# RWKV layer: the reversed copy of the values in DRAM made in two halves of eight column blocks, and the transposes of the key norms placed between two low-rank products

## The chip, the cores and the metric

The kernel runs on one core of one Trainium2 chip. The metric is the device time of one execution in microseconds (us). Three runs of the kernel before gave 2610.16, 2610.86 and 2616.23 us; the median is 2610.86 us.

## What is computed

One inference step of a four-layer backbone (retention, RWKV-7 time mixing, differential attention, neighbourhood attention) for 128 context tokens and 512 latent tokens, 640 in all, with 1024 channels in float32. Only the RWKV layer is touched. Cut to what matters, it is:

```python
r, k, v, g = einsum('nbld,dne->nble', stack([x_r, x_k, x_v, x_g]), w_in)   # x_* = h + (shift(h) - h) * mu[n]
kk = k * k_k
kk = kk * rsqrt(max(sum(kk * kk, -1), 1e-12))            # one root per token and head
for dr in range(2):                                      # forward and backward in time
    wlog = -softplus(-(w0[dr] + tanh(x_w @ wA[dr]) @ wB[dr])) - 0.5   # low-rank product
    a = sigmoid(a0[dr] + (x_a @ aA[dr]) @ aB[dr])                     # low-rank product
    kd = k * (1 + (a - 1) * k_a)
    seq = (r, exp(-exp(wlog)), kd, v, kk, a)
    if dr == 1:
        seq = tuple(flip(t, axis=time) for t in seq)     # the values are needed in reversed time too
    y_d, s_d = rwkv7_scan(*seq, s0[:, dr])
```

The values are needed twice: in the order of time for the forward scan, and reversed for the backward scan, apart for the 128 context tokens and the 512 latent tokens.

## The kernel before, in words

The RWKV layer has two stages. The first (`rwkv_project`, about 700 to 1180 us of the profile) makes the projections k, r, v and g in this order and stores them in DRAM; between k and r it makes the two low-rank products (`low_rank(1)` of tanh, `low_rank(4)`). The second (`rwkv_mix`) reads them back by pairs of heads and runs the scans in chunks of 64 tokens.

A projection goes through four column groups (`c2`, 256 columns each). Each group loads its weights in two DMAs of 512 KB (L160), which ScalarE (ACT) and VectorE (DVE) split into two parts each, and TensorE (PE) makes three products for each block of 128 inputs (L88 to L90). For the values, a group has five blocks of 128 tokens (`tt`); each result is copied by ACT from PSUM to one of two buffers `wvs` (L1149) and stored to the DRAM tensor `wd_v` (L1150). When the four groups of the values are done, two DMAs copy `wd_v` to `wd_vr` with reversed time, the 128 context tokens and the 512 latent ones apart (L1179). Both sides of the copy are seen as two column blocks of 512 columns (2 KB), the block first: 2 x 128 x 512 and 2 x 512 x 512. `wd_vr` is read by the second stage alone (L1477 to L1479).

The sums of squares of the keys land in a PSUM tile `wn` (L1173); DVE makes the roots (a tile of 128 x 80: 16 heads for each of five token blocks) in eleven small instructions (`rsqrt`, L124 to L129), PE turns them by five transposes (L1189), ACT copies them (L1190), and a DMA stores them to `wd_n` (L1191), from where each head pair reads its row into `wkk` (L1226) for the product in L1235.

While r, v and g are projected, a generator (`rwkv_prepare`, 8 steps, one per head pair) is fed into the same engines by priorities: it loads `wBr` (L1230), splits it into `wB` on ACT and DVE (L1232, L93), makes the decays, and stores `wd_bk`, `wd_q`, `wd_lt`, `wd_lb`; `rwkv_inverse` makes triangular inverses on DVE (L1310, L1312).

All engines run their instructions in a fixed order, which a scheduler works out from priorities and a simulated timeline; `high_priority()` moves what is inside it ahead. All DMAs are issued by SyncE (SP) in one order. A DMA's instruction waits in that order for its source and its target to be ready.

Of the kernel before, what the change touches and what calls it, by code (L numbers as in the profile page):

```python
# [7 lines left out]
F32 = mybir.dt.float32  # L8
# [10 lines left out]
NP = 128  # L19
# [1053 lines left out]
class Rwkv:  # L1073
    def rwkv_project(s, hT, dr):

        nc, I = s.nc, s.I
        v, act, pe, gp = nc.vector, nc.scalar, nc.tensor, nc.gpsimd
        s.pj_bufs, s.wz_bufs = 3, 2
        with s.pool(name='w1', bufs=1) as w1, s.pool(name='w1p', bufs=1, space=PSUM) as pp:
            s.pp = pp  # L1080
            T = lambda shape, name, bufs=1, dt=F32: w1.tile(shape, dt, name=name, tag=name, bufs=bufs)
            xx = T([128, 8, NT], 'wxx')

            for k, shape in (('wN', [80, 32, 32]), ('wX', [80, 32, 32]), ('wBK', [128, NCH, 128]), ('wQ', [128, 2, NCH, 64]),
                             ('wLT', [128, NCH, 64]), ('wt1', [128, NT]), ('wt2', [128, NT]), ('wt4', [128, NT])):
                T(shape, k, s.pbufs.get(k, 1))
            for a, b in PARTS:
                for g in range(0, 8, s.xx_g):
                    e = gp if s.xx_p[g // s.xx_g] == 'p' else v
                    lo, hi = max(a - 1, 1), b - 1  # L1090
                    G = slice(g, g + s.xx_g)
                    edge = lambda t, src: e.tensor_copy(xx[:, G, t:t + 1], hT[:, G, src:src + 1])
                    e.tensor_tensor(out=xx[:, G, lo:hi], in0=hT[:, G, lo - 1:hi - 1], in1=hT[:, G, lo + 1:hi + 1], op=ALU.add)
                    if a == 0:
                        edge(0, 1)
                        edge(NP - 1, NP - 2)
                        edge(NP, NP + 1)
                    else:
                        edge(NT - 1, NT - 2)
                    lo, hi = (0, hi) if a == 0 else (lo, NT)  # L1100
                    v.scalar_tensor_tensor(out=xx[:, G, lo:hi], in0=xx[:, G, lo:hi], scalar=0.5, in1=hT[:, G, lo:hi], op0=ALU.mult, op1=ALU.subtract)

            def mix(n, cuts=(0, NT)):
                parts = [(T([128, NT], 'wxh', s.x_bufs, F32R), T([128, NT], 'wxl', s.x_bufs, F32R)) for _ in range(8)]
                for a, b in zip(cuts, cuts[1:]):
                    for kc in range(8):
                        m = T([128, NT], 'wm', 2)[:, :b - a]
                        v.scalar_tensor_tensor(out=m, in0=xx[:, kc, a:b], scalar=s.vc('rwkv_mu', 8 * n + kc), in1=hT[:, kc, a:b],
                                               op0=ALU.mult, op1=ALU.add)
                        s.split(*(p[:, a:b] for p in parts[kc]), m, v)  # L1110
                return lambda kc, sl: (parts[kc][0][:, sl], parts[kc][1][:, sl])

            def low_rank(n, W, parts_, fn):
                x_ = mix(n)
                w = s.weights_list([W[0], W[1]])
                for hf in range(2):
                    ps = s.proj_T(w, 0, hf, x_)
                    t = T([128, HV], 'wlr')
                    act.activation(out=t, in_=ps, func=fn)
                    s.split(parts_[0][:, hf * HV:hf * HV + HV], parts_[1][:, hf * HV:hf * HV + HV], t)  # L1120

            W = I['rwkv_w_in'][0]
            nrm = pp.tile([128, 2, 512], F32, name='wn', tag='wn')

            for k, n in (('pj', s.pj_bufs), ('pm', 1), ('wz', s.wz_bufs)):
                for _ in range(n):
                    pp.tile([128, 512], F32, name=k, tag=k, bufs=n)
            prep = None

            def step(kind, c2):  # L1130
                for _ in range(s.preps.get(kind, (0, 0, 0, 0))[c2]):
                    with s.tc.high_priority(s.hp[4]):
                        next(prep)

            for n, base, kind in ((2, 1024, 'k'), (0, 0, 'r'), (3, 2048, 'v'), (5, 3072, 'g')):
                if kind == 'g' and s.rate:
                    s.fill_rest()
                x_ = mix(n, (0, HV, NT) if kind == 'k' else (0, NT))
                if prep is None:
                    s.tw = [T([128, NT], f'wtw{j}', 1, F32R) for j in range(2)]  # L1140
                    s.ta = [T([128, NT], f'wta{j}', 1, F32R) for j in range(2)]
                    prep = s.rwkv_prepare(w1, pp, dr)
                    next(prep)
                for c2 in range(4):
                    w = s.weights(W[:, base + c2 * 256:base + c2 * 256 + 256])
                    if kind == 'v':
                        for tt in range(5):
                            st = T([128, 256], 'wvs', 2)
                            act.copy(st, s.proj_N(w, tt, 256, x_))  # L1149
                            nc.sync.dma_start(out=dr['v'][tt * 128:tt * 128 + 128, c2 * 256:c2 * 256 + 256], in_=st)  # L1150
                        step('v', c2)
                        continue
                    sts = [T([128, NT], 'wst', 2) for _ in range(2)]
                    if kind == 'k':
                        sqs = [T([128, NT], k) for k in ('wt1', 'wt2')]
                    for hf in range(2):
                        for cc in range(2):
                            c, st = c2 * 2 + cc, sts[cc]
                            ps = s.proj_T(w, cc, hf, x_)
                            sl = slice(hf * HV, hf * HV + HV)  # L1160
                            if kind == 'g':
                                th = T([128, HV], 'wth')
                                act.activation(out=th, in_=ps, func=AF.Tanh, scale=0.5)
                                v.scalar_tensor_tensor(out=st[:, sl], in0=th, scalar=1.0, in1=ps, op0=ALU.add, op1=ALU.mult)  # L1164
                            else:
                                act.copy(st[:, sl], ps)
                                if kind == 'k':
                                    act.activation(out=sqs[cc][:, sl], in_=ps, func=AF.Square, scale=s.vc('rwkv_kk', c))
                    for cc in range(2):
                        if kind == 'k':  # L1170
                            c = c2 * 2 + cc
                            for tt in range(5):
                                pe.matmul(nrm[:, 0, tt * 16:tt * 16 + 16], sqs[cc][:, tt * 128:tt * 128 + 128], s.ind[:, c, :], start=c + tt == 0, stop=c + tt == 11)  # L1173
                        nc.sync.dma_start(out=dr[kind][c2 * 2 + cc], in_=sts[cc])
                    if kind in 'rg':
                        step(kind, c2)
                if kind == 'v':
                    for a, b in ((0, NP), (NP, NT)):
                        nc.sync.dma_start(out=dr['vr'][a:b].rearrange("t (a w) -> a t w", a=2),  # L1179
                                          in_=dr['v'][a:b].rearrange("t (a w) -> a t w", a=2)[:, ::-1])  # L1180
                if kind == 'k':
                    n2, y_, t_ = (T([128, 80], k) for k in ('wn2', 'wny', 'wnt'))
                    v.tensor_scalar(out=n2, in0=nrm[:, 0, :80], scalar1=1e-12, scalar2=None, op0=ALU.max)
                    rn = s.rsqrt(w1, n2, None, None, y_, t_)
                    rt = T([128, NT], 'wst', 2)[:16]
                    for a, b in ((0, 4), (4, 5)):
                        ps = pp.tile([128, 512], F32, name='pj', tag='pj', bufs=s.pj_bufs)
                        for tt in range(a, b):
                            pe.transpose(ps[:16, (tt - a) * 128:(tt - a) * 128 + 128], rn[:, tt * 16:tt * 16 + 16], s.ident)  # L1189
                        act.copy(rt[:, a * 128:b * 128], ps[:16, :(b - a) * 128])  # L1190
                    nc.sync.dma_start(out=dr['n'], in_=rt)  # L1191
                    with s.tc.high_priority():
                        low_rank(1, I['rwkv_wA'][0], s.tw, AF.Tanh)
                        low_rank(4, I['rwkv_aA'][0], s.ta, AF.Copy)

    def rwkv_prepare(s, pool, pp, dr):
# [649 lines left out]
```

## Time and profile before

| | us |
|---|---|
| median of three runs | 2610.86 |
| profiled execution | 2608.0 |
| its span | 2606.2 |
| PE busy / DVE busy / ACT busy | 2308.8 / 1500.5 / 1067.3 |
| mean granted clock of PE | 0.925 of full speed |

The page cuts the span into 40 slices of 65 us and gives each a digit of busy tenths. From slice 13 to slice 24 (782 to 1564 us) PE stands at 8 or 9 tenths, but for two: slice 17 (1042 to 1108 us) with 2 tenths of PE, 3 of DVE, 1 of ACT and a granted clock of 6 tenths, and slice 19 (1173 to 1238 us), where the second stage begins, with 4 tenths of PE and of DVE.

### The profile page before, as it was taken

The page shows a single profiled execution, that of the slowest core. Times are in us where ns is not written, and L with a number is a line of the kernel's source. Part 1 is how long each engine was busy: PE and PEld are TensorE (multiplying, and loading weights), DVE is VectorE, ACT ScalarE, POOL GpSimd, SP SyncE. Part 2 cuts the span into 40 slices and gives each one's busy share as a digit, 9 for nine tenths or more (in the row PEclk, how much of TensorE's full clock was granted, in tenths as well). Part 3 has the DMA queues.
Part 4 walks back from the last instruction along what each step waited for, and adds up shares of the span by engine and source line. Part 5 has one row for each costly group of instructions (what it writes and reads, how often), then busy time and mean ns, then how long its engine had stood idle before and what let it go on. Part 6 is the DMA issues. An engine that isn't in the chain of part 4 may idle for free.

```text
span 2606.2 us, 48698 instructions
## 1 busy us (share of the span) xinstructions
PE 2308.8 (89%) x18951; PEld 2086.3 (80%) x18951; DVE 1500.5 (58%) x3511; ACT 1067.3 (41%) x2405; POOL 675.5 (26%) x576
## 2 busy tenths in 40 slices
PE   7999999997988999294888997889889888999998
PEld 5888888987958889194777877688888887898888
DVE  7534343443173898394888554657776665645554
ACT  5323233332153655152333342245554433645551
POOL 3323232303210000001243433233222323332321
PEclk9999999998988889695888888899999998999999
DMA  8433333225272566367365645511111122223321
GB/s 294 131 101 102 118 101 110 90 85 188 83 262 69 166 191 216 107 193 182 102 148 136 160 126 177 175 56 48 45 55 39 51 68 56 67 76 78 77 71 57
DMA packets 344586, 303.54 MB, mean 116 GB/s; under 512 B 140220, under 2 KB 281044, under 8 KB 344356
## 3 DMA queue, kind: packets, MB, share of 16 engines
q1 hardware_dynamic: 344356, 300.44, 38.8%
q8 instruction: 149, 2.44, 0.4%
q14 instruction: 81, 0.66, 0.1%
HBM read 231.37 MB, written 64.79 MB: 114 GB/s over the span
## 4 chain that ended last, share of the span: by engine, by line
PE 34%; DVE 14%; DMA 4%; issue 3%; ACT 3%; SPq 3%; POOL 1%; ACTq 0%; DVEq 0%; POOLq 0%
PE pj L88 5%; PE pj L89 5%; PE pj L90 5%; PE oa L88 2%; PE oa L89 2%; PE oa L90 2%; DVE wtmp L1310 2%; DVE wX L1312 1%; PE nO L1024 1%; PE wsc L1439 1%; PE dtp L839 1%; PE wch L1507 1%; PE npt L1007 1%; PE wy L1541 1%; SPq L160 1%
## 5 line engine op out<-in xcount | busy, mean ns | idle before, releaser
L93 POOL TENSOR_TENSOR wl<-wr,wh 128x1024 fp32r<-128x1024 f32 (+1 forms) x168 | 371.2, 2222 | 628.5 <-ACT wh L170 490.4
L88 PE MATMUL pj<-hH,wh 128*128 128x320 f32 x1280 | 408.2, 321 | 10.5 <-ACT hH L96 7.1
L89 PE MATMUL pj<-hL,wh 128*128 128x320 f32 x1280 | 406.7, 318 | 3.0 <-POOL hL L93 2.4
L90 PE MATMUL pj<-hH,wl 128*128 128x320 f32 x1280 | 404.1, 316 | 0.1
L88 PEld LDWEIGHTS pj<-hH,wh 128*128 128x128 f32 x1280 | 246.4, 193 | 24.3 <-ACT hH L96 10.4
L89 PEld LDWEIGHTS pj<-hL,wh 128*128 128x128 f32 x1280 | 247.1, 193 | 10.6 <-POOL hL L93 3.8
L90 PEld LDWEIGHTS pj<-hH,wl 128*128 128x128 f32 x1280 | 246.5, 193 | 2.4 <-issue 1.0
L170 ACT CAST wh<-wr 128x1024 fp32r<-128x1024 f32 x168 | 175.5, 1047 | 133.7 <-PE pj L89 48.6
L88 PE MATMUL oa<-oh,wh 128*128 128x384 f32 (+1 forms) x640 | 201.6, 316 | 20.6 <-ACT wh L170 14.4
L89 PE MATMUL oa<-ol,wh 128*128 128x256 f32 (+1 forms) x640 | 199.3, 313 | 0.1
L88 PE MATMUL pj<-wh,hH 128*128 128x256 f32 x640 | 188.4, 294 | 12.2 <-DVE dr L756 7.4
L90 PE MATMUL oa<-oh,wl 128*128 128x256 f32 (+1 forms) x640 | 199.1, 312 | 0.0
L89 PE MATMUL pj<-wl,hH 128*128 128x256 f32 x640 | 186.0, 291 | 0.0
L90 PE MATMUL pj<-wh,hL 128*128 128x256 f32 x640 | 185.4, 290 | 0.0
L88 PE MATMUL pj<-wxh,wh 128*128 128x320 f32 x416 | 132.8, 327 | 53.2 <-DVE wst L1164 44.8
L88 PEld LDWEIGHTS pj<-wh,hH 128*128 128x128 f32 x640 | 127.5, 199 | 20.3 <-DVE dr L756 8.3
L88 PEld LDWEIGHTS oa<-oh,wh 128*128 128x128 f32 x640 | 122.8, 192 | 23.7 <-ACT wh L170 16.3
L89 PE MATMUL pj<-wxl,wh 128*128 128x320 f32 x416 | 134.5, 325 | 2.2 <-DVE wxl L93 2.2
L90 PE MATMUL pj<-wxh,wl 128*128 128x320 f32 x416 | 133.8, 323 | 1.9 <-DVE wl L93 1.9
L88 PEld LDWEIGHTS pj<-wxh,wh 128*128 128x128 f32 x416 | 82.1, 199 | 58.1 <-DVE wst L1164 45.1
L89 PEld LDWEIGHTS pj<-wl,hH 128*128 128x128 f32 x640 | 127.7, 200 | 0.0
L90 PEld LDWEIGHTS pj<-wh,hL 128*128 128x128 f32 x640 | 127.5, 199 | 0.0
(479 smaller groups left out, 5601.0 us busy)
## 6 DMA issues: line engine op xcount, KB each, us to landing
wr<-in_ret_w_in SPq DMA_DIRECT2D x48, 512.0 KB
wm<-in_w_mod SPq DMA_DIRECT2D x40, 512.0 KB
wr<-in_w_mod SPq DMA_DIRECT2D x32, 512.0 KB
wr<-in_rwkv_w_in SPq DMA_DIRECT2D x32, 512.0 KB
wl<-in_w_mod SPq DMA_DIRECT2D x24, 512.0 KB
wr<-in_diff_w_in SPq DMA_DIRECT2D x48, 256.0 KB
wr<-in_na_w_in SPq DMA_DIRECT2D x48, 256.0 KB
wd_bk<-wBK SPq DMA_DIRECT2D x16, 640.0 KB
```

The costliest lines, as they stand in the source:

```text
L88: mm(out, l[0], r[0], start=start, stop=False)
L89: mm(out, l[0], r[1], start=False, stop=False)
L90: mm(out, l[1], r[0], start=False, stop=stop)
L93: eng.tensor_tensor(out=lo, in0=src, in1=hi.bitcast(F32), op=ALU.subtract)
L160: nc.sync.dma_start(out=raw[:, :, c:c + x.shape[1]], in_=x[j * 128:(j + 4) * 128].rearrange("(k p) c -> p k c", p=128))
L170: nc.scalar.copy(hi[:, :, :n], raw[:, :, :n])
L839: pe.matmul(po, at[:, j * 128:j * 128 + 128], v_[:, vt, cc * 128:cc * 128 + 128], start=j == 0, stop=j == nt - 1)
L1007: pe.transpose(pt[:, j * 128:j * 128 + 128], P[:, j * 128:j * 128 + 128], s.ident)
L1024: pe.matmul(ot_ps[i * 64:i * 64 + 64, oc:oc + 128], vt[j][:, hc:hc + 64], pts[i][:, j * 128:j * 128 + 128], start=j == 0, stop=j == len(vt ...
L1310: v.tensor_tensor(out=t, in0=X_[:, 0:j + 1, j:j + 1].to_broadcast([80, j + 1, n]), in1=N_[:, j:j + 1, j + 1:].to_broadcast([80, j + 1, n]) ...
L1312: v.tensor_tensor(out=X_[:, 0:j + 1, j + 1:], in0=X_[:, 0:j + 1, j + 1:], in1=t, op=ALU.subtract)
L1439: pe.matmul(ps[:, u - u0, :], QT[:, u, :], TT[:, u, :], start=True, stop=True)
```

## The change

The copy to `wd_vr` is made in two halves of 512 columns: the first when the groups 0 and 1 of the values are done, the second when the groups 2 and 3 are done. Each half is seen as eight column blocks of 64 columns (256 bytes) instead of two of 512 columns; context and latent tokens stay apart, so there are four DMAs instead of two. The transposes of the keys' roots, ACT's copies of them and their store to `wd_n` are placed after `low_rank(1)` and before `low_rank(4)`, inside the same `high_priority()`.

```diff
@@ rwkv_project, in the loop over c2, kind 'v'
                             st = T([128, 256], 'wvs', 2)
                             act.copy(st, s.proj_N(w, tt, 256, x_))
                             nc.sync.dma_start(out=dr['v'][tt * 128:tt * 128 + 128, c2 * 256:c2 * 256 + 256], in_=st)
+                        if c2 % 2:
+
+                            hc = slice(c2 // 2 * 512, c2 // 2 * 512 + 512)
+                            for a, b in ((0, NP), (NP, NT)):
+                                blocks = [dr[k][a:b, hc].rearrange("t (a w) -> a t w", a=8) for k in ('vr', 'v')]
+                                nc.sync.dma_start(out=blocks[0], in_=blocks[1][:, ::-1])
                         step('v', c2)
                         continue
@@ after the loop over c2
-                if kind == 'v':
-                    for a, b in ((0, NP), (NP, NT)):
-                        nc.sync.dma_start(out=dr['vr'][a:b].rearrange("t (a w) -> a t w", a=2),
-                                          in_=dr['v'][a:b].rearrange("t (a w) -> a t w", a=2)[:, ::-1])
                 if kind == 'k':
                     n2, y_, t_ = (T([128, 80], k) for k in ('wn2', 'wny', 'wnt'))
                     v.tensor_scalar(out=n2, in0=nrm[:, 0, :80], scalar1=1e-12, scalar2=None, op0=ALU.max)
                     rn = s.rsqrt(w1, n2, None, None, y_, t_)
-                    rt = T([128, NT], 'wst', 2)[:16]
-                    for a, b in ((0, 4), (4, 5)):
-                        ps = pp.tile([128, 512], F32, name='pj', tag='pj', bufs=s.pj_bufs)
-                        for tt in range(a, b):
-                            pe.transpose(ps[:16, (tt - a) * 128:(tt - a) * 128 + 128], rn[:, tt * 16:tt * 16 + 16], s.ident)
-                        act.copy(rt[:, a * 128:b * 128], ps[:16, :(b - a) * 128])
-                    nc.sync.dma_start(out=dr['n'], in_=rt)
                     with s.tc.high_priority():
                         low_rank(1, I['rwkv_wA'][0], s.tw, AF.Tanh)
+                        rt = T([128, NT], 'wst', 2)[:16]
+                        for a, b in ((0, 4), (4, 5)):
+                            ps = pp.tile([128, 512], F32, name='pj', tag='pj', bufs=s.pj_bufs)
+                            for tt in range(a, b):
+                                pe.transpose(ps[:16, (tt - a) * 128:(tt - a) * 128 + 128], rn[:, tt * 16:tt * 16 + 16], s.ident)
+                            act.copy(rt[:, a * 128:b * 128], ps[:16, :(b - a) * 128])
+                        nc.sync.dma_start(out=dr['n'], in_=rt)
                         low_rank(4, I['rwkv_aA'][0], s.ta, AF.Copy)
```

The scheduler works the order of all engines out anew. Three places show what moved.

SP's order at the end of the values, before (`wd_v<-wvs` are the last stores of the values, `wr` weights of g, `wd_lt` and `wd_lb` stores of a head pair, `wBr` the load for the next one):

```order
L160 DMA wr<-in_rwkv_w_in 128x4x256
L1179 DMA wd_vr<-wd_v 2x128x512
L1286 DMA wd_lt_7686<-wLT 32x10x32 x2
L1287 DMA wd_lb_7694<-wLT 32x10x32
L1286 DMA wd_lt_7686<-wLT 32x10x32 x2
L1287 DMA wd_lb_7694<-wLT 32x10x32
L1150 DMA wd_v<-wvs 128x256 x3
L160 DMA wr<-in_rwkv_w_in 128x4x256
L1179 DMA wd_vr<-wd_v 2x512x512
L160 DMA wr<-in_rwkv_w_in 128x4x256
L1271 DMA wd_q_7671<-wQ 128x2x640
L1230 DMA wBr<-in_rwkv_aB 128x128
```

and the same place of SP's order after the change:

```order
L1288 DMA wd_lt_7686<-wLT 32x10x32 x2
L1289 DMA wd_lb_7694<-wLT 32x10x32
L1288 DMA wd_lt_7686<-wLT 32x10x32 x2
L1289 DMA wd_lb_7694<-wLT 32x10x32
L1150 DMA wd_v<-wvs 128x256 x2
L1156 DMA wd_vr<-wd_v 8x128x64
L1150 DMA wd_v<-wvs 128x256 x2
L160 DMA wr<-in_rwkv_w_in 128x4x256
L1156 DMA wd_vr<-wd_v 8x512x64
L160 DMA wr<-in_rwkv_w_in 128x4x256
L1273 DMA wd_q_7671<-wQ 128x2x640
L1232 DMA wBr<-in_rwkv_aB 128x128
```

The large copy stands at the same place, followed by the same three DMAs; it has half the bytes and eight blocks. The small copy has moved behind the four stores of `wd_lt` and the two of `wd_lb`.

SP's order in the third group of the values after the change, where the first half of the copy stands (before there is no copy here):

```order
L160 DMA wr<-in_rwkv_w_in 128x4x256 x2
L1288 DMA wd_lt_7685<-wLT 32x10x32 x2
L1289 DMA wd_lb_7693<-wLT 32x10x32
L1288 DMA wd_lt_7685<-wLT 32x10x32 x2
L1289 DMA wd_lb_7693<-wLT 32x10x32
L1156 DMA wd_vr<-wd_v 8x512x64
L1150 DMA wd_v<-wvs 128x256 x2
L1273 DMA wd_q_7670<-wQ 128x2x640
L1232 DMA wBr<-in_rwkv_aB 128x128
L1270 DMA wd_bk_7678<-wBK 128x1280
L160 DMA wr<-in_rwkv_w_in 128x4x256
L1150 DMA wd_v<-wvs 128x256 x2
```

Two stores of the values, a store `wd_q` and a load `wBr` come right behind the large copy of the first half.

PE's order at the roots before (`wn<-ind` are the sums of squares, `pj<-ident,wny` the transposes of the roots, `pj<-wxh,wh` the first product of `low_rank(1)`):

```order
L1173 MATMUL wn<-ind,wt_8383 128x16 x5
L1173 MATMUL wn<-ind,wt_8384 128x16 x5
L1189 MATMUL pj<-ident,wny 16x128 x5
L88 MATMUL pj<-wxh,wh 128x320
L89 MATMUL pj<-wxl,wh 128x320
```

and after the change:

```order
L89 MATMUL pj<-wxl,wh 128x320
L90 MATMUL pj<-wxh,wl 128x320
L88 MATMUL wz<-wtw_7880,wB_7922 128x320
L89 MATMUL wz<-wtw_7884,wB_7922 128x320
L90 MATMUL wz<-wtw_7880,wB_7926 128x320
L88 MATMUL wz<-wtw_7880,wB_7922 128x320
L89 MATMUL wz<-wtw_7884,wB_7922 128x320
L90 MATMUL wz<-wtw_7880,wB_7926 128x320
L1193 MATMUL pj<-ident,wny 16x128 x5
L88 MATMUL pj<-wxh,wh 128x320
```

The transposes now follow `low_rank(1)` and even the first six products of the decays (`wz<-wtw`) that use it; what follows them belongs to `low_rank(4)`.

## Rows read from the trace of the kernel before

**Rows 1.** Windows view, core 0: busy time by engine, PE clock, DMA share, GB/s.
```profile
core 0: us, PE busy (x) PEld busy (x) DVE busy (x) ACT busy (x) POOL busy (x), PEclk, DMA share, GB/s
860.00:920.00 60.00, 58.97 (x456) 56.53 (x457) 49.80 (x75) 38.46 (x84) 0.00 (x0) 0.92 0.54 172
...
980.00:1040.00 60.00, 57.55 (x556) 55.29 (x555) 49.74 (x94) 36.20 (x82) 1.12 (x2) 0.97 0.72 224
...
1060.00:1080.00 20.00, 1.36 (x16) 1.03 (x12) 0.89 (x2) 0.00 (x0) 0.00 (x0) 0.60 0.13 51
1080.00:1100.00 20.00, 0.00 (x0) 0.00 (x0) 0.62 (x3) 1.19 (x4) 0.00 (x0) 0.50 0.43 129
...
1160.00:1180.00 20.00, 15.44 (x138) 14.55 (x138) 20.00 (x45) 10.36 (x26) 3.07 (x6) 0.91 0.45 133
```

**Rows 2.** Waits of PE, 800 to 1250 us: who waited for what, total, times, longest.
```profile
PE pj L88 <- DVE wst L1164: 44.8, 1, 44.8
PE wtp L1422 <- DMA wKK<-wd_q: 18.0, 1, 18.0
PE pj L1189 <- DVE wny L129: 11.6, 1, 11.6
PE pj L88 <- ACT wvs L1149: 6.3, 1, 6.3
```

**Rows 3.** Timeline of SP: start, duration, DMA issued.
```profile
1033.71 0.69 SPq L1179 DMA_DIRECT2D wd_vr<-wd_v  x1
...
1051.04 0.61 SPq L1179 DMA_DIRECT2D wd_vr<-wd_v  x1
1051.75 33.14 SPq L160 DMA_DIRECT2D wr<-in_rwkv_w_in  x1
1084.99 4.62 SPq L1271 DMA_DIRECT2D wd_q<-wQ  x1
```

**Rows 4.** Timeline of ACT, 1048 to 1099 us: idle time before an instruction in brackets.
```profile
1048.74 0.37 ACT L1149 COPY wvs<-pj 128x256 f32<-128x256 f32 x1 [8.03 <-DMA wd_v<-wvs]
...
1057.88 0.53 ACT L1244 ACTIVATE wt<-wz,wha 128x320 f32<-128x320 f32 x1
1098.76 0.62 ACT L1232 CAST wB<-wBr 64x128 fp32r<-64x128 f32 x2 [40.35 <-DMA wBr<-in_rwkv_aB]
```

**Rows 5.** Chain that ended last, in order of time, 1048 to 1104 us.
```profile
1060.90 24.00 SPq L160
...
1089.70 9.03 DMA wBr<-in_rwkv_aB
```

**Rows 6.** DMA issues of the large copy: count, KB each.
```profile
wd_vr<-wd_v SPq DMA_DIRECT2D x1, 2048.0 KB
```

**Rows 7.** Windows view of four short stretches, each with one kind of DMA.
```profile
1066.00:1084.00 18.00, 0.00 (x0) 0.00 (x0) 0.00 (x0) 0.00 (x0) 0.00 (x0) 0.50 0.13 51
1213.00:1215.00 2.00, 1.43 (x34) 1.24 (x34) 0.89 (x2) 0.24 (x1) 0.00 (x0) 0.50 0.74 162
1385.00:1387.00 2.00, 0.72 (x8) 0.60 (x8) 1.37 (x6) 0.00 (x0) 0.62 (x2) 0.50 1.32 204
1099.00:1101.00 2.00, 0.00 (x0) 0.00 (x0) 1.62 (x4) 1.92 (x5) 0.00 (x0) 0.50 0.79 123
```

**Rows 8.** Timeline of PE, SP and DVE at the roots, 836 to 845 us.
```profile
836.14 1.23 PE L1189 MATMUL pj<-ident,wny 128*16 128x128 f32 x5 [11.57 <-DVE wny L129]
...
838.00 0.33 SPq L1191 DMA_DIRECT2D wd_n<-wst  x1
...
844.06 0.89 DVE L1235 SCALAR_TENSOR_TENSOR wkk<-wkk,wkkh,wk__8958 128x640 f32<-128x640 f32 x1 [7.97 <-DMA wkk<-wd_n]
```

**Rows 9.** Timeline of SP at the start of the second stage.
```profile
1183.74 0.60 SPq L1477 DMA_DIRECT2D wUV<-wd_v  x1
...
1192.66 0.62 SPq L1477 DMA_DIRECT2D wUV<-wd_v  x1
```

## The prediction, made before the changed kernel was timed

> **What bounds the kernel now.** I read the busy times by stage first. From 860 to 1040 us the projections are bound by PE: 58.97 of 60 us and 57.55 of 60 us, with DVE at 49.8 and 49.7 [rows 1]. Then comes a hole: from 1060 to 1100 us PE works 1.36 us, DVE 1.51 us, ACT 1.19 us and GpSimd nothing, while the DMA engines show a share of 0.13 in its first half [rows 1]. At the end of the stage DVE is the bound, 20.00 of 20 us [rows 1]. The waits of PE say the same from its side: one wait of 44.8 us, and after it three of 18.0, 11.6 and 6.3 us [rows 2]. The change touches three of the four.
>
> What fills the hole is read from SP and ACT. SP issues the large copy at 1051.04 us; the next DMA, weights of g, keeps it 33.14 us and the one after that 4.62 us, where an issue otherwise takes some 0.6 us [rows 3, 9]. The load `wBr` for the next head pair is issued only at 1089.70 and lands 9.03 us later, at 1098.73 [rows 5]. ACT runs out of work at 1058.41 and waits 40.35 us for it [rows 4]; DVE and then PE wait behind ACT, so the chain that ended last goes through SP's 24.00 us and this DMA [rows 5]. In the meantime the DMA engines move 51 GB/s at a share of 0.13 [rows 7]: 0.13 x 16 is two engines, each at 24.5 GB/s. The copy has 2048 KB [rows 6]; at 51 GB/s that is 41.1 us. So the copy runs on two of the 16 engines, as many as it has column blocks, and what has a part on those two stands behind it. `wBr` landed 47.7 us after the copy's issue: 41.1 us of copy and 6.6 us of everything else.
>
> The small copy (512 KB, a quarter, so 10.3 us) does the same at 1033.71 us on a smaller scale [rows 3]: ACT waits 8.03 us for a store of the values [rows 4] and PE 6.3 us [rows 2].
>
> **The change, part by part.** *The size of the copies.* Each half of the large copy has 1024 KB in rows of 256 bytes. If eight blocks mean eight engines, each moves 131 KB. Its rate is unknown for 256-byte rows from DRAM to DRAM; the nearest row is a stretch of 256-byte loads from DRAM: 162 GB/s at a share of 0.74, or 13.7 GB/s per engine [rows 7]. That makes 9.6 us. The bounds: 13.6 us at the 204 GB/s and 1.32 of a crowded stretch of such rows (9.7 GB/s per engine), and 5.3 us at the 24.5 GB/s of 2 KB rows [rows 7]. A small copy takes a quarter, 2.4 us. That eight blocks use eight engines is no row of before; the Trainium skill (DMA: Bandwidth & Descriptors, section "Why a DMA increments its semaphore by 16 and not by 1") says that a DMA is spread over the largest number up to 16 that divides the slowest dimension of both sides. By that rule 2 blocks give 2 engines, as the share of 0.13 shows, and 8 give 8.
>
> *The second half,* at the place of the large copy now, with the same three DMAs behind it in SP's order. `wBr` would land 9.6 + 6.6 = 16.2 us after the issue; ACT has 7.4 us of work (1051.04 to 1058.41) and waits 8.8 us instead of 40.35: 31.5 us saved (27.5 at the slow bound, 35.8 at the fast one). All engines stand in this hole, so what it gives back is time of the kernel; DVE's load after it stays as it is.
>
> *The small copy of the second half* blocks 2.4 us in place of 10.3, less than ACT's 8.03 us of wait shrinks by: PE's 6.3 us go (0 to 8).
>
> *The first half* is new in the third group of the values, with two stores of the values, a `wd_q` and a `wBr` behind it. Its 9.6 us are like the 10.3 us of the small copy now, which cost PE 6.3 us in the same stage. I charge 6.3 - 0.7 = 5.6 us: two buffers `wvs` cover the rest. It costs nothing if ACT has enough to do, and 9.6 us at the slow bound. Its small copy (2.4 us) is covered by these buffers. The two more issues of some 0.65 us each on SP [rows 3] lie beside PE's work.
>
> *The roots.* PE waits 11.57 us for the roots before the transposes, with `low_rank(1)` behind them [rows 8]. After the change PE goes on into `low_rank(1)` at once and the chain is set by DVE, which mixes the inputs of both low-rank products. DVE has 7.97 us of idle time of its own there, waiting for `wkk` from `wd_n` [rows 8]; in the new order L1235 stands behind most of the mixing for `low_rank(4)`. But `wd_n` is now stored later, after ACT's part of the first decay; from the store to L1235 it took 6.1 us (838.00 to 844.06) [rows 8]. I leave 1 us of the wait and take 7.0 us saved. Bounds: 11.6 us, and a loss of 2 us if `wkk` comes late. From there to 1040 us PE is the bound, so the lead is kept.
>
> *The order elsewhere.* The second stage's first loads move: between the last store of `wd_bk` and the first load `wKK`, for which PE waits 18.0 us [rows 2], SP has 34 DMAs instead of 26. Eight at 0.62 us [rows 9] are 5.0 us, but they are loads that would be issued a little later anyway; I charge half, 2.5 us (0 to 5.0). The layers after the second stage keep their order.
>
> Sum: 31.5 + 6.3 - 5.6 + 7.0 - 2.5 = 36.7 us. Against the profiled execution of 2608.0 us that is 2571.3; the median of the runs lies 2.9 us above that execution, and I take 2573. All bounds on one side give 27.5 + 0 - 9.6 - 2 - 5.0 = 10.9 us or 35.8 + 8 + 11.6 = 55.4 us, that is 2600 or 2555.
>
> **The rivals.** *Short rows at half rate.* The copy now writes 256-byte rows into DRAM. For it: no row of before copies such rows from DRAM to DRAM. Against: stores of 128-byte rows into DRAM (`wd_lt`) move 123 GB/s at a share of 0.79, 9.7 GB/s per engine [rows 7], 13 ns a row, so short stores alone show no collapse. At half of 13.7 GB/s a half takes 19.1 us: the second half still saves 40.35 - (19.1 + 6.6 - 7.4) = 22.0 us, the first costs 6.3 + 19.1 - 10.3 = 15.1, and with 6.3 + 7.0 - 2.5 from the other terms 17.7 us are left: 2593. The Trainium skill (DMA: Bandwidth & Descriptors, Specifications) speaks for this case: below 512 bytes it has the engine read, modify and write. No run here shows that for a copy inside DRAM.
>
> *A fixed price per row, slower than before.* If a row costs a time of its own, whatever its size, the cut into eight multiplies the rows. At the 84 ns of a 2 KB row (2048 bytes at 24.5 GB/s), 512 rows on an engine take 42.8 us in each half: the second half loses 1.6 us against now, the first 38.8 us in the middle of the values, its small part (10.7 us) another 6.7, and 4.5 come from roots and order: 2611 + 43 = 2653. The point from which it decides is where 41.1 - 0.512c for the second half, 4.0 - 0.512c for the first and 10.8 us for the rest sum to nothing: c = 55 ns a row. The rows of 256 bytes seen take 18.7 ns, 26.5 in the crowd [rows 7].
>
> *The copy stays on two engines.* Then 2048 rows of 18.7 ns stand on each in a half, 38 us; the second half saves 3 us, the first costs 34 and its small part 5.6: about 2643. Against it stands only that two blocks went with two engines.
>
> *More than the sum.* The scheduler's new order could take away part of the 18.0 us wait as well, or the clock, 0.50 in the hole [rows 1], may cost more after it than I count: 2545 to 2555.
>
> **How the numbers follow.** My forecast (2555 to 2584) has 0.70, short rows at half rate (2584 to 2600) 0.16, more than the sum 0.08, no gain that can be measured 0.02, the two slower ones together 0.04. A measurement of this kernel tells about 0.3% (8 us) from no change. Faster by more than that: 0.70 + 0.16 + 0.08 = 0.94; within it 0.02; slower 0.04. The range of 2553 to 2594 takes the forecast, most of the half-rate case and a little of the larger gain.
>
> **What would show it.** In the profile after, the hole from 1060 to 1100 us is gone: ACT's wait for `wBr` is under 15 us, SP's longest issue behind a copy under 10 us, and PE's waits no longer hold one of 44.8 us. While a large copy runs alone, the DMA share is near 0.5 and the rate near 110 GB/s. In the third group of the values a wait of ACT for a store `wd_v` of some 5 to 8 us is new. PE's 11.57 us before the transposes are gone and `low_rank(1)` ends some 10 us after the sums of squares. Wrong would be: a large copy of more than 15 us, a wait of PE of more than 12 us in the third or fourth group, or a first load `wKK` as late behind the last g as before plus 5 us.

## The result, and the profile after

The changed kernel took 2572.8 us (median of four runs, 2564.4 to 2575.1), the kernel before 2610.98 us on the same chip: ratio 0.9844 [0.9817, 0.987]. The forecast was 2573 us, its range 2553 to 2594. The profiled execution of the changed kernel took 2574.4 us (span 2572.6), that of before 2608.0 (span 2606.2). The ratios leave out three executions far slower than the others: one of the kernel before (2698 us) and two of the variant "the roots alone" (8.8 and 10.8 ms), whose median below still contains them.

Its windows by stage, with the columns of [rows 1]:

```profile
core 0: us, PE busy (x) PEld busy (x) DVE busy (x) ACT busy (x) POOL busy (x), PEclk, DMA share, GB/s
860.00:920.00 60.00, 58.42 (x498) 54.74 (x498) 46.59 (x67) 35.20 (x77) 0.00 (x0) 1.00 0.62 187
...
980.00:1040.00 60.00, 56.16 (x504) 53.47 (x505) 47.93 (x95) 33.48 (x74) 1.10 (x2) 0.91 0.78 229
...
1060.00:1080.00 20.00, 16.19 (x119) 15.45 (x120) 11.99 (x26) 10.81 (x23) 1.26 (x1) 0.76 0.95 255
1080.00:1100.00 20.00, 18.77 (x167) 17.46 (x166) 19.00 (x46) 12.97 (x31) 1.10 (x2) 1.00 0.65 197
...
1120.00:1140.00 20.00, 13.72 (x130) 12.51 (x129) 20.00 (x43) 10.29 (x27) 3.08 (x6) 0.86 0.49 146
```

From 1060 to 1100 us PE works 34.96 us where it worked 1.36: the hole is closed. The end of the stage, where DVE has no gap (20.00 of 20 us), comes 40 us earlier by the span's time.

Timeline of SP, as [rows 3]: the large copy of the first half and what follows it, then the large copy of the second.

```profile
1005.82 0.69 SPq L1156 DMA_DIRECT2D wd_vr<-wd_v  x1
1006.92 8.55 SPq L1150 DMA_DIRECT2D wd_v<-wvs  x2
...
1044.40 0.68 SPq L1156 DMA_DIRECT2D wd_vr<-wd_v  x1
1045.17 7.91 SPq L160 DMA_DIRECT2D wr<-in_rwkv_w_in  x1
1053.14 0.50 SPq L1273 DMA_DIRECT2D wd_q<-wQ  x1
1053.69 0.46 SPq L1232 DMA_DIRECT2D wBr<-in_rwkv_aB  x1
```

The 33.14 us of SP behind the copy have become 7.91, and the 4.62 behind those 0.50. The windows while the second half runs answer to [rows 7], and the row of ACT to [rows 4]:

```profile
1046.00:1048.00 2.00, 0.23 (x1) 0.23 (x2) 2.00 (x5) 0.56 (x1) 0.00 (x0) 1.00 0.58 135
1048.00:1050.00 2.00, 2.00 (x12) 2.00 (x12) 1.94 (x4) 0.09 (x1) 0.00 (x0) 0.74 0.56 128
```

```profile
1058.75 0.62 ACT L1234 CAST wB<-wBr 64x128 fp32r<-64x128 f32 x2 [3.41 <-DMA wBr<-in_rwkv_aB]
```

The share is 0.58 and 0.56 where it was 0.13, and ACT's wait is 3.41 us where it was 40.35. Waits of PE from 800 to 1250 us, with the columns of [rows 2]:

```profile
PE wtp L1424 <- DMA wKK<-wd_q: 23.3, 1, 23.3
PE wn L1282 <- ACT wLT L1283: 7.9, 6, 3.1
...
PE pj L1193 <- DVE wny L129: 4.3, 1, 4.3
```

The wait of 44.8 us is gone, that for the roots is 4.3 instead of 11.6, and the one for the first load of the second stage has grown from 18.0 to 23.3.

Milestones from SP's timelines put the difference of the two profiled executions in place (us; forecast by the terms of the prediction):

| stretch | before | after | difference | forecast |
|---|---|---|---|---|
| start to first store of the keys | 769.8 | 770.2 | +0.4 | 0 |
| to the issue of the last copy | 281.2 | 274.2 | -7.0 | -7.7 |
| to the last store `wd_bk` | 131.4 | 96.7 | -34.7 | -31.5 |
| to the first load `wKK` | 20.8 | 25.7 | +4.9 | +2.5 |
| to the end | 1403.0 | 1405.8 | +2.8 | 0 |
| sum | 2606.2 | 2572.6 | -33.6 | -36.7 |

### The profile page after: what moved, and what is told of

Same layout as the page of the kernel before. It is cut to its first block, busy times and chain, and to the rows that moved or that the text cites. A ratio compares the mean times of both kernels' runs of the same rounds, so it can differ in the third digit from the quotient of the medians.

```text
span 2572.6 us, 48694 instructions
## 1 busy us (share of the span) xinstructions
PE 2310.7 (90%) x18951; PEld 2081.0 (81%) x18951; DVE 1500.1 (58%) x3511; ACT 1072.4 (42%) x2405; POOL 673.9 (26%) x576
## 4 chain that ended last, share of the span: by engine, by line
PE 64%; DVE 18%; DMA 8%; ACT 4%; issue 4%; SPq 2%; POOL 1%; DVEq 0%; ACTq 0%; POOLq 0%
PE pj L88 11%; PE pj L89 11%; PE pj L90 11%; PE oa L88 3%; PE oa L89 3%; PE oa L90 3%; PE pm L326 2%; DVE wtmp L1312 2%; DVE wX L1314 2%; PE wsc L1441 2%; PE nO L1024 1%; PE ro L88 1%; PE ro L90 1%; PE ro L89 1%; PE dtp L839 1%
## 5 line engine op out<-in xcount | busy, mean ns | idle before, releaser
L89 PEld LDWEIGHTS pj<-hL,wh 128*128 128x128 f32 x1280 | 247.4, 193 | 10.8 <-POOL hL L93 4.1
L88 PE MATMUL oa<-oh,wh 128*128 128x384 f32 (+1 forms) x640 | 201.1, 315 | 20.8 <-ACT wh L170 14.6
L89 PEld LDWEIGHTS oa<-ol,wh 128*128 128x128 f32 x640 | 122.9, 192 | 0.9 <-DVE ol L93 0.7
```

Of the source, the lines that this page charges most:

```text
L88: mm(out, l[0], r[0], start=start, stop=False)
L89: mm(out, l[0], r[1], start=False, stop=False)
```

## The experiments

Three sets of four kernels, each set on one chip, with the kernel before beside it (2607.51, 2609.37 and 2608.64 us). All ratios are to it.

**The changed kernel again.** 

> The changed kernel once more, as the yardstick on this chip. Both theories: 2573 us, as recorded, within 0.3% (2565 to 2581).

Measured 2573.92 us, 0.9862 [0.9834, 0.9891]: as in the first comparison.

**The copies alone.** The halves in eight blocks; the roots stay where they were.

> Only the copies are changed; the transposes of the roots stand before both low-rank products, as before. Theory A (number of column blocks = number of DMA engines of the copy; the hole behind the copy is its time on an engine): the hole stays closed, ACT waits under 6 us for the load wBr after the last copy, and the lead of 5 us that the trace shows from the roots is lost: about 2578 us (2572 to 2585). Theory B (the two parts of the change only work together): above 2590 us.

Measured 2561.06 us, 0.9817 [0.9789, 0.9846]: a miss of 17 us, and faster than the whole change; the hole is closed as theory A has it (ACT waits 3.88 us for `wBr`). It was run again in the second set, below.

**The roots alone.** The move of the transposes, with the old copies in two blocks.

> Only the roots are moved; the copy is whole, in two blocks, after the last group, as before. Theory A: the hole of 40 us stays, PE's wait of 44.8 us too, and only the lead of the roots is gained: about 2606 us (2600 to 2611). Theory B: the roots carry a good part of the gain, below 2595 us.

Measured 2600.57 us, 0.9967 [0.9949, 0.9986]: theory A, some 7 us. PE's waits:

```profile
PE pj L88 <- DVE wst L1164: 36.2, 1, 36.2
PE wtp L1422 <- DMA wKK<-wd_q: 24.5, 1, 24.5
...
PE pj L1191 <- DVE wny L129: 4.4, 1, 4.4
```

The hole stays, though shorter than theory A had it (36.2 us, not 44.8), and the wait for the roots is as short as in the change.

**One whole copy in eight blocks.** The roots moved, no halves:

```diff
-   dr['vr'][a:b].rearrange("t (a w) -> a t w", a=2)    # likewise the source
+   dr['vr'][a:b].rearrange("t (a w) -> a t w", a=8)
```

> The copy is whole again, after the last group, but in eight blocks of 128 columns (rows of 512 bytes); the roots are moved as in the change. Theory A: 2048 KB on eight engines are 262 KB each, at about 19 GB/s (512 bytes in 27 ns) 13.8 us; ACT waits 13.8 + 6.6 - 7.4 = 13 us for wBr in place of 40.35, and the copy in the third group is gone: about 2579 us (2571 to 2587). Theory C (the halving is what counts, since the first half is out of the way early): above 2590 us.

Measured 2568.8 us, 0.9837 [0.9807, 0.9867]: no slower than the halves, and 2 us below the range of theory A; ACT waits 9.10 us for `wBr` where the theory had 13. Theory C is excluded. SP and the windows while the copy runs:

```profile
1045.74 0.66 SPq L1179 DMA_DIRECT2D wd_vr<-wd_v  x1
1046.50 10.73 SPq L160 DMA_DIRECT2D wr<-in_rwkv_w_in  x1
```

```profile
1049.00:1051.00 2.00, 1.99 (x28) 1.64 (x27) 2.00 (x5) 1.83 (x4) 1.94 (x3) 1.00 0.57 174
1051.00:1053.00 2.00, 1.78 (x27) 1.44 (x26) 2.00 (x3) 1.34 (x4) 0.02 (x1) 1.00 0.57 174
```

**Halves in two blocks.** The change with `a=2` in place of `a=8`.

> The changed kernel with its halves cut into two column blocks instead of eight (rows of 1024 bytes); roots moved as in the change. Theory A, the number of blocks sets the number of engines a copy uses: each half then stands on two engines with 524 KB each, at the 24.5 GB/s per engine of the old copy 21.4 us; wBr lands 21.4 + 6.6 = 28 us after the copy's issue and ACT waits about 20 us for it (3.4 in the changed kernel), the next issue of SP behind the copy takes 15 to 22 us instead of 7.9, and the first half now costs some 5 to 13 us in the third group: 2590 to 2606. Rival B, cutting the copy into halves is what counts, the first being hidden: ACT waits under 10 us, 2570 to 2582.

Measured 2596.18 us, 0.9955 [0.994, 0.9969]: theory A, with a wait of ACT for `wBr` of 20.34 us. SP behind the second half, and a window:

```profile
1066.78 0.62 SPq L1156 DMA_DIRECT2D wd_vr<-wd_v  x1
1067.68 17.65 SPq L1348 DMA_DIRECT2D wmask<-in_const_rwkv_mask  x1
```

```profile
1072.00:1080.00 8.00, 2.29 (x30) 1.77 (x28) 2.97 (x6) 1.35 (x3) 0.00 (x0) 0.84 0.14 48
```

The share is 0.14 again. The first half now does cost time in the third group: ACT waits 16.60 us for a store of the values, PE 14.9. The way from the first store of the values to the issue of the last copy is 105.8 us where the changed kernel has 81.6: 24.2 us more, where the theory allowed 5 to 13 for the first half.

```profile
1034.89 0.72 ACT L1149 COPY wvs<-pj 128x256 f32<-128x256 f32 x2 [16.60 <-DMA wd_v<-wvs]
```

**One whole copy in sixteen blocks.** As the whole copy above, with `a=16`.

> One whole copy after the last store of the values, as in the kernel before, but in sixteen column blocks (rows of 256 bytes); roots moved as in the change. Theory A, the copy's time is the bytes per engine: 128 KB on each of 16 engines, 7.5 to 9.6 us, as long as a half in eight blocks; ACT's wait for wBr 6 to 9 us (9.1 with eight blocks of 512 bytes), DMA share near 1.0 while the copy runs alone, 2564 to 2573. Rival B, a copy over all 16 engines holds up every other transfer and gives the gain back: stores and wd_q loads behind it late, 2576 to 2590.

Measured 2567.97 us, 0.9836 [0.9813, 0.986]: theory A; nothing behind the copy is late, and ACT waits only 1.97 us for `wBr`, less than the theory's 6 to 9. SP and a window:

```profile
1043.82 7.20 SPq L160 DMA_DIRECT2D wr<-in_rwkv_w_in  x1
```

```profile
1047.00:1049.00 2.00, 1.99 (x28) 1.76 (x28) 2.00 (x4) 1.95 (x5) 1.86 (x3) 1.00 1.28 289
```

**The old kernel with eight blocks.** Only `a=2` to `a=8`; roots as before.

> The kernel before with one number changed: the whole copy in eight column blocks instead of two; roots where they were. Theory A, the block count brings all of the gain and the move of the roots nothing or a loss, because its one wait of 11.6 us comes back as many short waits of the low-rank mixing: 2554 to 2567. Rival B, the move of the roots is worth 7 us here too, as it was with the old copy: 2572 to 2580.

Measured 2576.34 us, 0.9888 [0.9869, 0.9907]: the time of rival B. By the medians this one number brings 0.0112 of the 0.0156 of the whole change, and moving the roots beside it 0.0051 more (0.9837). By the stretches in the table at the end of this section it brings all of it, and the move next to nothing: theory A in the mechanism. PE's waits here:

```profile
PE wtp L1422 <- DMA wKK<-wd_q: 17.4, 1, 17.4
PE pj L88 <- DVE wst L1164: 13.2, 1, 13.2
PE pj L1189 <- DVE wny L129: 11.6, 1, 11.6
```

**The copies alone, once more.**

> The halves in eight blocks with the roots left where they were, once more. Theory A, leaving the roots alone is worth some 10 us beside the new copies: 2556 to 2566, and the RWKV stage from the first store of the keys to the last store of the diffusion cache is again 5 to 8 us shorter than in the changed kernel (1242.8 us). Rival B, the first result came from a better granted clock in later layers (0.91 to 1.00 from 2005 to 2078 us, 0.85 to 0.92 in the same work of the changed kernel): 2568 to 2575, and the 8 us between the last store of the diffusion cache and the first of the neighbourhood cache (122.8 against 130.2) are gone.

Measured 2569.15 us, 0.9848 [0.9829, 0.9867], where the change has 0.9844 and 0.9862: that leaving the roots alone is worth 10 us did not hold. But neither theory holds whole. From the first store of the keys to the last store of the diffusion cache it took 1240.3 us, only 2.5 less than the changed kernel (theory A: 5 to 8). And the second sign of rival B failed: from the last store of the diffusion cache to the first of the neighbourhood cache it again took 123.0 us (122.8 in the first run, 130.2 in the changed kernel). The order goes with this difference: PE's order in the later layers is all but the same in all kernels, but on DVE, some 360 us ahead of this stretch, a few rows of the modulation stand in another order (two of `h<-t,mod` ahead of a `mod<-pj,vec`, another `mod<-pj,vec` behind a rotation instead of ahead of it). The four profiled executions with these rows (the copies alone twice, the halves in two blocks, no copy) take 122.4 to 127.5 us for the stretch, the ten others, before and after among them, 128.6 to 132.2. The granted clock differs in a part of it; 19 us of the changed kernel, and, equally far behind the last store of the diffusion cache, 19 us of the copies alone in their first run:

```profile
2031.00:2050.00 19.00, 13.17 (x65) 11.59 (x63) 10.33 (x29) 5.35 (x15) 4.17 (x3) 0.91 0.18 55
```

```profile
2023.00:2042.00 19.00, 14.83 (x88) 12.64 (x86) 14.48 (x37) 7.74 (x24) 3.96 (x2) 1.00 0.18 55
```

But the clock does not sort the kernels: over the whole stretch it is 0.91 in the changed kernel and 0.94 and 0.93 with the copies alone, yet 0.94 with the roots alone (129.4 us) and 0.91 without a copy (127.5 us). So some 7 us by which the copies alone lead the change in the profiled executions lie in work a thousand microseconds behind the edit. That the order of the rows causes them is argued from which kernels have it, not shown.

**The old copies from another queue.** One word in the kernel before:

```diff
-   nc.sync.dma_start(out=dr['vr'][a:b]...
+   nc.scalar.dma_start(out=dr['vr'][a:b]...
```

> The kernel before with one word changed: the two copies, whole and in two blocks as they were, are issued by ACT instead of SP; roots where they were. Theory A, what costs the time is that SP's order stands still behind the copy, its next DMAs finding no room on the two busy engines: SP's issues behind the copy then take under 3 us (33.14 before), wBr is issued at once and ACT waits under 12 us for it; the copy itself still takes some 40 us but nobody needs it yet: 2570 to 2582, as eight blocks gave without the roots (2576). Rival B, the load wBr has to wait for the two busy engines whichever queue it stands in: ACT still waits 25 to 40 us, 2598 to 2612.

Measured 2624.61 us, 1.0055 [1.0033, 1.0077]: both theories missed, and the kernel is slower. A to the letter holds at first: behind ACT's copy, issued at 1048.45, SP issues five DMAs in 0.3 to 0.7 us each, and `wBr` is there after a wait of 0.90 us. Then SP stops.

```profile
1050.87 0.68 SPq L1230 DMA_DIRECT2D wBr<-in_rwkv_aB  x1
1051.60 0.50 SPq L1383 DMA_DIRECT2D wLB<-wd_lb  x1
1052.15 0.41 SPq L1384 DMA_DIRECT2D wTM<-wd_tq  x1
1052.61 0.50 SPq L1383 DMA_DIRECT2D wLB<-wd_lb  x1
1096.23 0.30 SPq L1384 DMA_DIRECT2D wTM<-wd_tq  x1
```

The waits of SP, of ACT for `wBr`, and of DVE in the same stretch:

```profile
SPq L1384 <- DMA wd_vr<-wd_v: 43.1, 1, 43.1
```

```profile
1056.38 0.62 ACT L1232 CAST wB<-wBr 64x128 fp32r<-64x128 f32 x2 [0.90 <-DMA wBr<-in_rwkv_aB]
```

```profile
1103.10 1.56 DVE L1265 TENSOR_TENSOR wBK<-wt,wt 128x640 f32<-128x640 f32 x2 [39.71 <-DMA wd_bk<-wBK]
```

This is a wait that the program holds. Its order numbers the DMAs through eight semaphores (DMAHW0 to DMAHW7), and each DMA first waits for the DMA that had its semaphore before it. The copy stands between the first two of these rows and has DMAHW6, and so has the load that stops, the eighth of SP's DMAs behind it:

```
476 L160 DMA wr<-in_rwkv_w_in 128x4x256 [waits DMAHW5_49,DVE_49]
477 L160 DMA wr<-in_rwkv_w_in 128x4x256 [waits DMAHW7_49,DVE_49]
...
484 L1384 DMA wTM<-wd_tq_7706 32x20x32 [waits DMAHW6_49]
```

So in this program a copy of over 40 us stops SP at the eighth DMA behind it even from another queue, and DVE then waits 39.71 us for a buffer of `wd_bk` where ACT had waited 40.35 for `wBr`: the hole has moved, not closed. Of the 15.4 us by which the profiled execution is longer than that of before, 13.2 lie behind the first load `wKK` and were not explained.

**The eight-block copy from another queue.** The same word in the whole copy in eight blocks, roots moved.

> The whole copy in eight blocks with the roots moved (2568.8 us in an earlier set), now issued by ACT instead of SP. Theory A, what is left of the hole is SP's order standing behind the copy: ACT's wait for wBr falls from 9.1 to under 4 us and PE's wait for wst from 9.9 to under 4: 2558 to 2566. Rival B, what is left is the transfer time on the shared engines, or is made good elsewhere: 2566 to 2574.

Measured 2569.41 us, 0.9844 [0.9819, 0.9868]: rival B, no gain over SP's queue (0.9837). Theory A's signs came, for ACT's wait for `wBr` and PE's for `wst` are under the 4 us that it named, but its time did not: PE now waits 15.3 us for `wBK` (9.1 with SP's queue). The same load again waits for the copy, now 14.2 us:

```profile
SPq L1384 <- DMA wd_vr<-wd_v: 14.2, 1, 14.2
```

**Halves in sixteen blocks.** The change with `a=16`, rows of 128 bytes.

> The changed kernel with its halves in sixteen blocks instead of eight (rows of 128 bytes, 64 KB on each of 16 engines). Theory A, a row has a price of its own of some 15 ns, whatever its size below 256 bytes: 512 rows, 7.7 us, as in the changed kernel; the issue behind the copy again takes 7 to 9 us, 2568 to 2577. Rival B, the price goes by bytes (17 GB/s on an engine): 3.9 us, the issue behind the copy 3 to 5 us, 2562 to 2569. Rival C, rows below a size run at half rate or worse: 15 us or more, the issue behind it over 13 us, 2580 to 2595.

Measured 2574.98 us, 0.9862 [0.9836, 0.9887]: as the change, and the time of theory A; C is excluded. The issue behind the second half lies between A and B:

```profile
1048.53 6.37 SPq L160 DMA_DIRECT2D wr<-in_rwkv_w_in  x1
```

**No copy.** The change without its copies.

> The changed kernel without any copy: the backward scan reads the values as they were stored, so the reversal of the values is left out; all else as in the change. Theory A, two copies in eight blocks still cost some 8 to 12 us (two stretches in which SP's order stands for 8 us each): ACT's wait for wBr under 2 us, 2558 to 2566. Rival B, in eight blocks the copy is hidden to within what can be told: 2567 to 2575.

Measured 2548.78 us, 0.9768 [0.9742, 0.9794]: below both theories. In the profiled executions the way from the first store of the keys to the last `wd_bk` is 8.0 us shorter than in the changed kernel (362.9 against 371.0), the lower end of A's 8 to 12, and from there to the first `wKK` 4.5 (21.1 against 25.7). The profiled execution (2559.25 us) is the slowest of the five; the rest of the 24 us between the medians was not placed.

Of the variants that keep a copy, none is told apart from the change as faster by its times.

**By stretch.** The profiled executions, cut at the first load `wKK`, place these differences (us; two numbers are two executions of one kernel):

| kernel | first store of the keys to first `wKK` | from there to the end |
|---|---|---|
| before | 433.4 | 1403.0 |
| changed kernel | 396.6, 396.9 | 1405.8, 1407.6 |
| the copies alone | 392.4, 396.5 | 1395.1, 1396.6 |
| the roots alone | 426.6 | 1401.2 |
| whole copy in eight blocks, roots moved | 395.8 | 1399.9 |
| whole copy in eight blocks, old roots | 396.5 | 1405.4 |
| whole copy in sixteen blocks, roots moved | 389.5 | 1405.6 |
| halves in two blocks | 431.8 | 1394.5 |
| halves in sixteen blocks | 396.6 | 1411.4 |

The stage that the edits change lies in the first column, where two executions of one kernel differ by 0.3 and 4.1 us. There the one number `a=8` in the old kernel brings 36.9 us, as much as the whole change (36.8); sixteen blocks bring 7 more in their one execution, which the times do not tell apart. The second column, over work whose instructions none of these edits changes (the scheduler orders them anew), differs by up to 17 us, and much of what parts the medians of the variants lies there.

## Why the prediction was right

**The second half (31.5 us saved).** Right in mechanism, and a little undersized: the stretch behind the copy fell by 34.7 us and ACT's wait by 36.9 (40.35 to 3.41). Two things were too careful. The rate: the 128 GB/s of the second window above are 16.0 on each of eight engines, against 13.7 in the forecast; SP was free 7.9 us after it stood, not 9.6, and `wBr` was there 14.3 us after the copy's issue, not 16.2. And ACT's other work: it ran out 10.9 us after the issue, not 7.4, which is the larger part. One reading went too far without costing anything: that what has a part on the two engines stands behind the copy. With the copy in ACT's queue `wBr` passed it and ACT waited 0.90 us; what stood was SP's own order. The runs give a row of every size while a copy runs:

| copy | engines by share | GB/s | issue behind it, us |
|---|---|---|---|
| whole, 2 blocks, 2048 B rows [rows 3, 7] | 0.13 x 16 = 2.1 | 51 | 33.14 |
| half, 2 blocks, 1024 B | 0.14 x 16 = 2.2 | 48 | 17.65 |
| whole, 8 blocks, 512 B | 0.57 x 16 = 9.1 | 174 | 10.73 |
| half, 8 blocks, 256 B | 0.56 x 16 = 9.0 | 128 | 7.91 |
| whole, 16 blocks, 256 B | 1.28 x 16 = 20.5 | 289 | 7.20 |
| half, 16 blocks, 128 B | 1.20 x 16 = 19.2 | 189 | 6.37 |

The share sums the times of packets, and a share of 1.28 says that they overlap on an engine; so it is 1.0 to 1.3 for each block, and no row names the engines themselves.

The Trainium skill (DMA: Bandwidth & Descriptors, section "Why a DMA increments its semaphore by 16 and not by 1") has the number of engines follow the slowest dimension; shares that grow with two, eight and sixteen blocks (0.13, 0.57, 1.28) agree with it.

**Halves or blocks.** The prediction did not part the two. The runs do: halves in two blocks keep 0.9955, the whole copy in eight 0.9837, and in sixteen 0.9836. The blocks bring the gain; with the roots moved, halving on top of eight blocks brings nothing (395.8 us without the halves, 396.6 and 396.9 with them, to the first `wKK`).

**The small copy (6.3 us).** With the roots moved, the way from the first store of the values to the last copy's issue is 85.6 us with the old copy and 80.2 with eight blocks: 5.4 us. With the old roots it is 83.8 and 76.0: 7.8 us.

**The first half (5.6 us charged).** Too dear. The wait of ACT for a store of 5 to 8 us that was to show it did not come (0.52 and 0.72 us are the longest in the third and fourth group), and the same stretch is 81.6 us with halves against 80.2 without, 77.8 against 76.0 with the old roots. The two buffers cover 8.55 us of SP. They did not cover the half in two blocks, behind which SP's stores of the values took 18.35 us: there the term appears, with 14.9 us of PE.

**The roots (7.0 us).** Right beside the old copy, where the way to the first `wKK` falls by 6.8 us (433.4 to 426.6). Beside the new copies next to nothing came: 396.5 without the move and 395.8 with it for the whole copy, 392.4 and 396.5 against 396.6 and 396.9 for the halves. The medians agree for the halves (0.9817 and 0.9848 without it, 0.9844 and 0.9862 with it); the 0.0051 that they show beside the whole copy lie, in the profiled executions, for the most part behind `wKK` (1405.4 against 1399.9). The prediction said that PE goes into `low_rank(1)` at once, and that the lead is kept because PE is the bound to 1040 us. The trace after:

```profile
834.44 0.39 PE L88 MATMUL wz<-wtw,wB 128*128 128x320 f32 x1 [2.24 <-ACT wtw L96]
835.91 0.42 PE L89 MATMUL wz<-wtw,wB 128*128 128x320 f32 x1 [1.09 <-DVE wtw L93]
...
838.95 0.63 PE L89 MATMUL wz<-wtw,wB 128*128 128x320 f32 x1 [1.59 <-DVE wtw L93]
```

PE does go in, but waits there for ACT and DVE in pieces, and with the 4.3 us for the roots behind them 9.2 of the 11.57 us are back. Counted from the first store of the keys, the first store of r comes 4.7 us earlier (105.8 for 110.5), of v 4.8 us; in the second execution of the changed kernel 3.8 and 3.2. Beside the new copies this lead is gone by the last copy (274.4 us with the roots moved, 272.6 without, whole copy in eight blocks), since the values' groups take 4.2 us longer (80.2 against 76.0). Their windows, with the move and without:

```profile
965.57:1045.74 80.17, 78.55 (x703) 76.33 (x702) 71.19 (x133) 49.32 (x113) 1.11 (x2) 0.95 0.69 207
```

```profile
969.31:1045.31 76.00, 73.90 (x687) 71.34 (x687) 65.83 (x125) 46.91 (x106) 1.10 (x2) 0.99 0.70 212
```

PE is the bound in both, as forecast, but with the move it makes 16 products more, and its granted clock is 0.95 instead of 0.99 (1.00 is 2.4 GHz throughout, 0.50 is 1.2). An estimate from these two rows gives some 3 us to the clock (78.55 x (1 - 0.95 / 0.99) = 3.2). With the halves it is 0.93 and 0.94 with the move, 0.98 and 0.97 without. From the last copy to the last `wd_bk` the move then gains 6.0 us (97.5 against 103.5), and loses 3.5 again before the first `wKK` (23.9 against 20.3). The step that failed is "the lead is kept". Why the clock is lower after the move was not tried.

**The order (2.5 us charged).** 4.9 us measured, at the upper bound of 5.0; PE's wait for `wKK` grew by 5.3 (18.0 to 23.3). The first `wKK` came 26.4 us behind the last store of g, 22.3 before: 4.1 later, short of the 5 that would have spoken against the prediction.

**The sum.** The forecast met the median to 0.2 us, and the stretch from the first store of the keys to the first `wKK` fell by 36.8 us where the sum has 36.7. That closeness is luck: the roots' 7.0 us did not come in the change, the order cost 2.4 us more than charged, and against these stand some 4 us too many charged for the first half and 3.2 too few for the second. The main term, six sevenths of the sum, was right by its mechanism.

**The rivals.** *Short rows at half rate:* at 256 bytes a sixteenth of 289 GB/s is 18.1 GB/s for an engine, above the 13.7 taken; at 512 an eighth of 174 is 21.8. That is no halving, so the rule of the Trainium skill cited for it (DMA: Bandwidth & Descriptors, Specifications) does not show in these rates. Rows of 128 bytes cost a half no more time only because they ran on twice the engines: a sixteenth of 189 is 11.8 GB/s. *A fixed price per row:* the half in eight blocks has 512 rows on an engine and holds SP for 7.91 us, 15 ns a row, and a row of 2048 bytes takes 80 (25.5 GB/s on each of two engines), so the price is not fixed; the point from which the rival decides was 55. *Two engines still:* the share is 0.56, not 0.13. *More than the sum:* no.

## What to carry to other kernels

The DRAM copy whose outer dimension is 2 ran on two DMA engines, and what stood still was not the copy's reader but the order of the queue behind it: read the issue that follows a large DMA, and cut the outer dimension first; here one number gave the whole gain of its stage. A copy moved to another queue does not free the order if the DMAs share a ring of semaphores: count the DMAs until its semaphore comes round. And variants that differ early in this kernel differed by up to 17 us in later work that no edit touched, so a few microseconds between two of them are to be placed by stretch before they are put down to the edit.

## What was not expected of the hardware

Copies inside DRAM with rows of 256 bytes ran at 289 GB/s on sixteen engines (18.1 GB/s on each) where 2048-byte rows on two gave 51 (25.5 on each): cutting the row to an eighth cost under a third of an engine's rate. The next halving, to 128 bytes, cost another third (11.8). While a copy filled two engines from ACT's queue, five DMAs of SP's queue passed in 0.3 to 0.7 us each; behind the same copy in SP's own queue the first one took 33.14 us.
